# The 32 modulation products and their loads, moved from the convolutions into the attention

## The chip, the cores and the metric

The kernel runs on one core of a Trainium2 chip. The metric is the device time of one execution in microseconds (us), taken as the median of several runs. Beside the runs, one execution was recorded by the hardware profiler, and everything said below about where time goes comes from that record. The engines are TensorE (PE for its matmuls, PEld for its weight loads), VectorE (DVE), ScalarE (ACT), GpSimd (POOL) and SyncE (SP), whose instruction queue issues almost all DMA loads. [...]

## The reference, cut to what matters

One layer of a streaming encoder over 1024 positions of width 1024, in float32: an RMSNorm with modulation, a state-space (SSD) branch and a chunked attention branch side by side, an output projection with a gate, a second modulated norm and a convolutional feed-forward network with a gate.

```python
c_act = jax.nn.silu(c)
mod = (c_act @ w_ada[l] + b_ada[l])[:, None, :]
sh_m, sc_m, g_m, sh_f, sc_f, g_f = jnp.split(mod, 6, axis=-1)
h = rmsnorm(x, norm_mix_w[l]) * (1 + sc_m) + sh_m
z, xbc, dt_raw, q, k, v = jnp.split(h @ w_in[l], IN_SPLITS, axis=-1)
y_ssd = ssd_mixer(z, xbc, dt_raw, ...)
y_att = chunk_attention(q, k, v, rel_bias[l])
x = x + g_m * (jnp.concatenate([y_ssd, y_att], axis=-1) @ w_out[l])
h = rmsnorm(x, norm_ffn_w[l]) * (1 + sc_f) + sh_f
x = x + g_f * conv_ffn(h, w_up[l], ffn_conv_w[l], w_down[l])
```

The row of interest is `mod`: a vector of 1024 times a matrix of 1024 x 6144. Its six parts are two shifts, two scales and two gates. The first norm needs `sh_m` and `sc_m`; the other four (`g_m`, `sh_f`, `sc_f`, `g_f`) are needed only much later, the gate of the output projection first.

## The kernel before, in words

Every large product is made from pairs of numbers: a value is split into a rounded high part and a remainder (`split`, lines 60 to 66), and `mm3` (lines 55 to 58) adds three matmuls. `split` puts the high part on ACT (L65) and the remainder on DVE or POOL (L66).

**The modulation.** The vector by matrix product isn't made on TensorE. `w_ada` is stored as 48 blocks of 128 output columns by 1024; `mod_col(ft, t)` loads block `ft` (512 KB) into a tile `t` (L112, on SP's queue) and multiplies it on DVE with the activated `c`, held as a row in all partitions (`rowa`), summing along the row into one column of `modc` (L113). `mod_scale` and `mod_shift` (L168 to L174) turn a column into the scale `affn` and the shift `bffn` with three operations on 128 x 1 elements. Sixteen blocks (`sh_m`, `sc_m`) are done at the start, tile names `adat`. The other 32, tile name `mt`, are those of this change: 24 stand in `mods(kt)` after each of the eight convolutions, and the last eight (`g_f`) follow ahead of the z projection.

**The stages around the change**, with their places in the profiled execution:

- The first projection (to about 100 us) makes q, k and v of head pairs 0 and 1.
- The attention (about 100 to 325 us). `attention(p)` handles a pair of heads in four steps u, of two query blocks each. `attn_scores` makes the scores of one block in PSUM (L305, tile `s`, two buffers, one for each head), then per head one DVE operation that adds the bias and takes the row maximum (L317, tile `p`), the exponential on ACT (L320), and on DVE a reciprocal (L322) and the scaling (L323). `attn_pv` transposes the result on PE (L349, L352, tile `tp`), splits it (tile `pt`), multiplies by v (L360, L361, tile `pv`) and adds on DVE (L366, tile `ya`). The projections of pairs 2 and 3 (`gemm_part`, tile `acc`, six parts of 48 matmuls) are given as work between: three parts in pair 1, three in pair 2. Their weights are loaded into `raws` (L128) and split by ACT and POOL. Pairs 0 and 3 have no such part written into them.
- The convolutions (`conv_silu`, about 280 to 394 us): eight projections of 48 matmuls into the `s` tiles, each followed by ACT (L411) and three DVE operations that read the `s` tile (L413), and two more DVE operations (L419). The `s` tile is free for the next projection but one when these are done.
- The z projection (`z_tile`, tiles `zps` and `s`, about 384 to 442 us) with weights `wzh`, `wzl` made by ACT and DVE (L62, L63), the rows of the two gates (`row_of`, L120 to L124), the step sizes (`dt_prep`) and the first chunk of the SSD (`ssd_pre`, tiles `cb`, `rm`, `th`).
- Then the SSD chunks and the output projection (to about 600 us), and the feed-forward network.

**What sets the order.** A scheduler takes the instructions in the order in which they are written, estimates when each could run, and writes one list for each engine. Priorities follow the written order; a pin (`tc.issue_after(ins)`) forces an instruction behind `ins` in the list of that engine and adds no wait. The tiles `mt` come from a pool of three buffers (`MTB`), in memory that the attention's tiles hold before.

## Time and profile before

| | |
|---|---|
| median of 3 runs | 1265.64 us (1264.97 to 1270.69) |
| the profiled execution's own time | 1264.52 us |
| its span, first to last instruction | 1262.8 us |
| PE busy, DVE busy, ACT busy, POOL busy | 95%, 77%, 44%, 8% of the span |
| mean granted TensorE clock | 0.987 |
| the 32 products `mt` | first issue of a load at 326.3 us, last product at 415.7 us |

A row of the groups gives line, engine, operation, tile names, shapes and count, then busy us, mean ns of one, and the idle time of the engine before them with what ended it. A row of the waits reads: who waited, for whom, us in total, times, longest. A row of the windows gives, for a stretch from A to B, its length, the busy us of PE, PEld, DVE, ACT and POOL with their counts, the granted clock, the DMA share and GB/s. A row of the timeline gives start, length, engine, line, operation and tiles. "PE busy" counts a matmul until its modelled end, so a stretch in which matmuls wait can still look busy.

### The profile page before, as it was taken

What the parts mean: (1) busy time and instruction counts of PE and PEld (TensorE: products, weight loads), DVE (VectorE), ACT (ScalarE), POOL (GpSimd) and SP (SyncE); (2) the same over time, 40 slices, a digit from 0 to 9 for tenths busy, and PEclk for the clock granted to TensorE, in tenths of its full rate; (3) what the DMA queues carried; (4) which work ended last, traced back from release to release, by engine and by line L of the source; (5) the groups of instructions that cost most, each with busy time, mean ns of one, the idle gap of its engine ahead of it and who ended that gap; (6) DMA issues with size and microseconds to landing.
All of it is one profiled execution on the core that took longest, in us unless ns stands there. A gap on an engine that the chain in (4) does not pass through costs nothing.

```text
span 1262.8 us, 15592 instructions
## 1 busy us (share of the span) xinstructions
PE 1194.4 (95%) x5882; PEld 991.1 (78%) x5882; DVE 975.9 (77%) x1517; ACT 550.7 (44%) x901; POOL 105.2 (8%) x114
## 2 busy tenths in 40 slices
PE   5899999999999879999799999999999999999995
PEld 3777888878779768888578888888888888888884
DVE  7827665584797986664989898888998879856976
ACT  4516454563323443434634444443344435443443
POOL 1300201001200242310000000000000000000002
PEclk9999999899999989999999999999999999999998
DMA  9601110001574422212213323223322186834433
GB/s 341 245 1 42 42 42 33 29 1 34 186 249 150 133 84 67 67 67 67 89 46 125 125 75 108 92 100 126 125 76 106 75 311 217 301 108 140 160 125 133
DMA packets 55275, 146.67 MB, mean 116 GB/s; under 512 B 5280, under 2 KB 5408, under 8 KB 53792
## 3 DMA queue, kind: packets, MB, share of 16 engines
q1 hardware_dynamic: 48144, 121.30, 28.2%
q10 hardware_dynamic: 7056, 24.38, 4.8%
q8 instruction: 46, 0.75, 0.2%
q14 instruction: 29, 0.24, 0.1%
HBM read 116.56 MB, written 29.10 MB: 115 GB/s over the span
## 4 chain that ended last, share of the span: by engine, by line
PE 80%; DVE 13%; DMA 3%; ACT 2%; issue 1%; POOL 1%; DVEq 0%; POOLq 0%; SPq 0%; ACTq 0%
PE dn L57 6%; PE dn L56 6%; PE dn L58 5%; PE uY L56 5%; PE uY L58 5%; PE uY L57 5%; PE acc L57 3%; PE acc L56 3%; PE uZ L58 3%; PE uZ L56 3%; PE uZ L57 3%; PE acc L58 3%; PE uX L58 3%; PE uX L56 3%; PE uX L57 3%; PE s L305 3%
## 5 line engine op out<-in xcount | busy, mean ns | idle before, releaser
L56 PE MATMUL dn<-w 128*128 128x512 f32 x308 | 111.9, 389 | 0.0
L57 PE MATMUL dn<-w 128*128 128x512 f32 x308 | 111.9, 389 | 0.0
L58 PE MATMUL dn<-w 128*128 128x512 f32 x308 | 103.3, 389 | 0.0
L65 ACT ACTIVATE w<-ya 128x1024 fp32r<-128x1024 f32 (+1 forms) x44 | 41.8, 949 | 99.6 <-PE uY L58 92.2
L763 POOL TENSOR_TENSOR st<-st,mhalf 128x1 f32<-128x1 f32 x16 | 12.4, 777 | 680.0 <-DVE st L762 680.0
L56 PEld LDWEIGHTS dn<-w 128*128 128x128 f32 x308 | 57.8, 188 | 12.0
L58 PEld LDWEIGHTS dn<-w 128*128 128x128 f32 x308 | 57.8, 188 | 12.0
L57 PEld LDWEIGHTS dn<-w 128*128 128x128 f32 x308 | 57.8, 188 | 11.9
L66 DVE TENSOR_TENSOR pt<-tp,pt 128x512 fp32r<-128x512 f32 (+2 forms) x72 | 42.2, 595 | 28.1 <-ACT pt L65 28.0
L65 ACT ACTIVATE w<-xs 128x1024 fp32r<-128x1024 f32 (+1 forms) x44 | 41.8, 951 | 40.6 <-PE uY L58 31.6
L65 ACT ACTIVATE pt<-tp 128x512 fp32r<-128x512 f32 (+2 forms) x72 | 36.6, 523 | 45.6 <-PE tp L349 16.4
L56 PE MATMUL s<-hth,wh 128*128 128x512 f32 x128 | 50.8, 397 | 4.4 <-DVE xst L413 2.2
L317 DVE CUSTOM_DVE_ANT_0 p<-s,bias 128x640 f32<-128x640 f32 (+4 forms) x64 | 40.4, 649 | 16.2 <-PE tp L352 7.5
L66 DVE TENSOR_TENSOR w<-ya,w 128x1024 fp32r<-128x1024 f32 (+1 forms) x44 | 47.7, 1084 | 4.5 <-ACT w L65 4.5
L905 DVE SCALAR_TENSOR_TENSOR a<-cv,pkt,a 128x1023 f32<-128x1023 f32 (+1 forms) x40 | 51.0, 1276 | 0.1
L57 PE MATMUL s<-htl,wh 128*128 128x512 f32 x128 | 50.4, 394 | 0.0
L58 PE MATMUL s<-hth,wl 128*128 128x512 f32 x128 | 50.2, 392 | 0.0
L66 POOL TENSOR_TENSOR wl<-raws,wh 128x1024 fp32r<-128x1024 f32 x14 | 34.3, 2454 | 185.8 <-ACT wh L65 168.2
L320 ACT ACTIVATE p<-p,st 128x640 f32<-128x640 f32 (+4 forms) x64 | 44.1, 690 | 12.9 <-DVE st L317 12.6
L905 DVE SCALAR_TENSOR_TENSOR a<-cg,pkt,a 128x1023 f32<-128x1023 f32 (+1 forms) x40 | 49.5, 1276 | 0.0
L305 PE MATMUL s<-qk 64*128 64x320 f32 (+4 forms) x288 | 47.6, 340 | 0.3 <-DVE st L317 0.2
L66 DVE TENSOR_TENSOR w<-xs,w 128x1024 fp32r<-128x1024 f32 (+1 forms) x44 | 47.6, 1081 | 0.0
(407 smaller groups left out, 3583.4 us busy)
## 6 DMA issues: line engine op xcount, KB each, us to landing
mt<-in_w_ada_dram SPq DMA_DIRECT2D x32, 512.0 KB, 4.2
gz<-a ACTq DMA_DIRECT2D x10, 1024.0 KB, 5.2
adat<-in_w_ada_dram SPq DMA_DIRECT2D x16, 512.0 KB, 5.9
ya<-in_w_up_dram SPq DMA_DIRECT2D x10, 768.0 KB, 4.0
xs<-in_w_up_dram SPq DMA_DIRECT2D x10, 768.0 KB, 4.1
raws<-in_w_ft_dram SPq DMA_DIRECT2D x14, 512.0 KB, 3.5
gy<-a ACTq DMA_DIRECT2D x10, 512.0 KB, 2.6
qk<-in_x_dram SPq DMA_DIRECT2D x8, 512.0 KB, 6.0
```

What stands on the lines that cost most here:

```text
L56: T.matmul(ps, lh, rh, start=start, stop=False, skip_group_check=more)
L57: T.matmul(ps, lh, rl, start=False, stop=False, skip_group_check=more)
L58: T.matmul(ps, ll, rh, start=False, stop=stop, skip_group_check=more)
L65: i = A.activation(hi, src, AF.Copy) if ehi is A else ehi.tensor_copy(hi, src)
L66: return i, elo.tensor_tensor(lo, src, f32(hi), ALU.subtract)
L305: T.matmul(st[h][:, 512 * pi:512 * pi + w], d[qn][r, i * P:(i + 1) * P], d[kn][r, j0 * P + a:j0 * P + a + w], start=ti == 0, stop=ti == 2)
L317: V.tensor_tensor_reduce(out=dst, in0=src, in1=bsl, scale=-1.0, scalar=3e38, op0=ALU.add, op1=ALU.min, accum_out=nm)
L320: A.activation(pv_, pv_, AF.Exp, scale=-1.0, bias=nm, accum_out=rs)
L763: G.tensor_tensor(r, ms, mhalf[:, 0:1], ALU.pow)
L905: V.scalar_tensor_tensor(a[:, j:S], c[:, 0:S - j], w[2 - j], a[:, j:S], op0=ALU.mult, op1=ALU.add)
```

## The change

`mods` and its pool move from the convolution stage into the attention. In each step u of each pair, after the two heads' `attn_pv`, two columns are done: pair p and steps 0 and 1 do the four columns of `kt` = 2p (scale and shift, then the two gates), steps 2 and 3 those of `kt` = 2p + 1. That makes eight in each pair and 32 in all. Each load is pinned in SP's list behind the second bias load of its pair (`sp`), each product in DVE's list behind the last softmax scaling of its step (`last_v`). The pool now stands on the left side of the memory, where its first three loads wait for no other tile, and is closed with the attention. The eight `g_f` columns no longer use the `rm` tiles. No computation is added or dropped.

```diff
--- before.py
+++ after.py
@@ -108,10 +108,13 @@
         rawc[0] += 1
         return raws[:, rawc[0] % 2, 0:n]
 
-    def mod_col(ft, t):
-        nc.sync.dma_start(t, w_ada[ft])
-        V.tensor_tensor_reduce(out=t, in0=t, in1=rowa, scale=1.0, scalar=0.0,
-                               op0=ALU.mult, op1=ALU.add, accum_out=modc[:, ft:ft + 1])
+    def mod_col(ft, t, at=None):
+        sp, v = at or (None, None)
+        with tc.issue_after(sp) if sp else ExitStack():
+            nc.sync.dma_start(t, w_ada[ft])
+        with tc.issue_after(v) if v else ExitStack():
+            V.tensor_tensor_reduce(out=t, in0=t, in1=rowa, scale=1.0, scalar=0.0,
+                                   op0=ALU.mult, op1=ALU.add, accum_out=modc[:, ft:ft + 1])
 
     def row_of(cols, dst, psp, tag, bufs, ones, tmp):
         for hh in range(2):
@@ -320,7 +323,7 @@
             A.activation(pv_, pv_, AF.Exp, scale=-1.0, bias=nm, accum_out=rs)
             rr = stat()
             V.reciprocal(rr, rs)
-            V.tensor_scalar(pv_, pv_, rr, None, op0=ALU.mult)
+            last_v[:] = [V.tensor_scalar(pv_, pv_, rr, None, op0=ALU.mult).ins]
             res.append(pt_)
         return res
 
@@ -367,12 +370,14 @@
                         pv[0:64, :].rearrange("p (a b) -> p a b", a=2),
                         tl.rearrange("p (a b) -> p a b", a=2), ALU.add)
 
+    last_v = []
+
     def attention(p, extra=()):
         extra = dict(extra)
         bt = []
         for h in range(2):
             t = bp.tile([P, 640], F32, tag="bias", name="bias")
-            nc.sync.dma_start(t, bias[2 * p + h])
+            sp = nc.sync.dma_start(t, bias[2 * p + h]).ins
             G.memset(t[0:64, 576:640], -1e30)
             G.memset(t[64:128, 0:64], -1e30)
             bt.append(t)
@@ -383,6 +388,7 @@
                 fn()
             for h in range(2):
                 attn_pv(p, u, h, pa[h], pb[h])
+            mods(2 * p + u // 2, u % 2, (sp, last_v[0]))
 
     def gemm_ft(wh, wl, outs, rh, rl):
         for hh in range(2):
@@ -418,6 +424,22 @@
             A.activation(th, dst[:, c], AF.Tanh)
             V.scalar_tensor_tensor(dst[:, c], th, 1.0, dst[:, c], op0=ALU.add, op1=ALU.mult)
 
+    es_m = ExitStack()
+    mtp = es_m.enter_context(tc.tile_pool(name="mtp", bufs=1, side="left", reuse_waits="tile"))
+
+    def mt_tile():
+        return mtp.tile([P, D], F32, tag="mt", bufs=MTB, name="mt")
+
+    def mods(kt, part, at):
+        if part == 0:
+            mod_col(SC_F + kt, mt_tile(), at)
+            mod_scale(affn, SC_F, NFFN, kt)
+            mod_col(SH_F + kt, mt_tile(), at)
+            mod_shift(bffn, SH_F, kt)
+        else:
+            mod_col(G_M + kt, mt_tile(), at)
+            mod_col(G_F + kt, mt_tile(), at)
+
     part = lambda p, w: (lambda: gemm_part(p, w))
     attention(0)
     for p in (1, 2):
@@ -425,6 +447,7 @@
         for w in GPL:
             gemm_part(p + 1, w)
     attention(3)
+    es_m.close()
     es_at.close()
 
 
@@ -463,28 +486,12 @@
     sgt = f32(sgtr)
     na = bcp.tile([P, 16], F32, name="na")[:, 0:8]
     es_t = ExitStack()
-    es_m = ExitStack()
-    mtp = es_m.enter_context(tc.tile_pool(name="mtp", bufs=1, side="right", reuse_waits="tile"))
-
-    def mt_tile():
-        return mtp.tile([P, D], F32, tag="mt", bufs=MTB, name="mt")
-
-    def mods(kt):
-        mod_col(G_M + kt, mt_tile())
-        mod_col(SC_F + kt, mt_tile())
-        mod_scale(affn, SC_F, NFFN, kt)
-        mod_col(SH_F + kt, mt_tile())
-        mod_shift(bffn, SH_F, kt)
-
     for g in range(2):
         conv_silu(4 + g, bt_[g], th512)
-        mods(2 * g)
         conv_silu(6 + g, ct_[g], th512)
-        mods(2 * g + 1)
     for ft in range(4):
         xt = bcp.tile([P, S], F32, tag="rm", bufs=2, name="xst")
         conv_silu(ft, xt, th512)
-        mods(4 + ft)
         for hh in range(2):
             tps = tp_tile()
             for j in range(4):
@@ -514,8 +521,6 @@
             split(wh, wl, t, A, V)
             ws += [(wh[:, 0:512], wl[:, 0:512]), (wh[:, 512:1024], wl[:, 512:1024])]
         return ws
-
-    es_m.close()
 
     def rm512():
         return bcp.tile([P, S], F32, tag="rm", bufs=2, name="gt")[:, 0:512]
@@ -577,8 +582,6 @@
             T.matmul(dps[:, 64 * i:64 * i + 64], m, sm["adt"], start=True, stop=True)
         A.activation(ex3, dps[:, 0:192], AF.Exp)
 
-    for kt in range(KT):
-        mod_col(G_F + kt, bcp.tile([P, S], F32, tag="rm", bufs=2, name="mt"))
     def hb(n, c):
         return sm[n][:, c * 8:c * 8 + 8].unsqueeze(2).to_broadcast([P, 8, 64])
 
```

Three places show what this does to the lists. Line numbers of the changed kernel are 3 higher from the middle of the helpers on and 5 higher in the attention: L116 is the product (L113 before), L320 the maximum (L317), L325 and L326 reciprocal and scaling (L322, L323), L114 the load `mt` (L112), L380 the load of the bias (L375), L131 the load of projection weights (L128).

**DVE, pair 0 of the attention, from the second block's reciprocals to the fourth block's maximum.** Before:

```order
L322 RECIPROCAL st_72<-st_72 128x1
L323 TENSOR_SCALAR p<-p,st_72 128x256
L317 ISA p,st_72<-s,bias 128x384
L317 ISA st_72 128x1
L317 ISA p,st_72<-s,bias 128x384
L317 ISA st_72 128x1
L66 TENSOR_TENSOR pt<-tp,pt 128x384
L317 ISA p,st_72<-s,bias 128x512
```

And now:

```order
L325 RECIPROCAL st_72<-st_72 128x1
L326 TENSOR_SCALAR p<-p,st_72 128x256
L116 ISA mt,modc<-mt,rows 128x1024
L116 ISA modc 128x1
L116 ISA mt,modc<-mt,rows 128x1024
L116 ISA modc 128x1
L320 ISA p,st_72<-s,bias 128x384
L320 ISA st_72 128x1
L320 ISA p,st_72<-s,bias 128x384
L320 ISA st_72 128x1
L66 TENSOR_TENSOR pt<-tp,pt 128x384
L171 TENSOR_TENSOR st_72<-modc,pkt 128x1
```

Two products and one read of the sum each now stand between the scaling of a step's second block (256 columns) and the maximum of the next step's first block (384 columns) before the list went straight from the scaling to the maximum. The operations on `st` and `bffn` (L171, L177 and L173, three for a `kt`) follow the products a few places later.

**SP's list from the bias loads of pair 0 on**, where `raws` are the projection weights and `mt` the modulation blocks. Before:

```order
L128 DMA raws<-in_w_ft_dram 128x1024 x4
L375 DMA bias<-in_bias_dram 128x640 x5
L128 DMA raws<-in_w_ft_dram 128x1024 x3
L375 DMA bias<-in_bias_dram 128x640 x2
L128 DMA raws<-in_w_ft_dram 128x1024 x3
L375 DMA bias<-in_bias_dram 128x640
```

And now:

```order
L131 DMA raws<-in_w_ft_dram 128x1024 x4
L380 DMA bias<-in_bias_dram 128x640 x2
L114 DMA mt<-in_w_ada_dram 128x1024 x3
L380 DMA bias<-in_bias_dram 128x640
L114 DMA mt<-in_w_ada_dram 128x1024 x5
L380 DMA bias<-in_bias_dram 128x640
L114 DMA mt<-in_w_ada_dram 128x1024
L380 DMA bias<-in_bias_dram 128x640
L114 DMA mt<-in_w_ada_dram 128x1024 x2
L131 DMA raws<-in_w_ft_dram 128x1024
L114 DMA mt<-in_w_ada_dram 128x1024 x4
L131 DMA raws<-in_w_ft_dram 128x1024
```

The weight loads that followed each other, held only by their own buffers, now have up to five `mt` loads ahead of them in the same list, and so has a pair's second bias load.

**DVE in the convolutions**, where L413 and L419 are the three products and the last step of a convolution before the change (L419 and L425 after it), `ct` and `xst` its results. Before:

```order
L413 SCALAR_TENSOR_TENSOR ct_2777<-s,pkt,ct_2777 128x1023
L170 SCALAR_TENSOR_TENSOR affn<-st_72,pkt 128x1
L113 ISA mt,modc<-mt,rows 128x1024
L113 ISA modc 128x1
L113 ISA mt,modc<-mt,rows 128x1024
L113 ISA modc 128x1
L413 SCALAR_TENSOR_TENSOR ct_2777<-s,pkt,ct_2777 128x1022
L168 TENSOR_TENSOR st_72<-modc,pkt 128x1
L174 TENSOR_TENSOR bffn<-modc,pkt 128x1
L113 ISA mt,modc<-mt,rows 128x1024
L113 ISA modc 128x1
L413 SCALAR_TENSOR_TENSOR ct_2777<-s,pkt,ct_2777 128x1021
```

And now:

```order
L419 SCALAR_TENSOR_TENSOR xst<-s,pkt,xst 128x1022
L419 SCALAR_TENSOR_TENSOR xst<-s,pkt,xst 128x1021
L63 SCALAR_TENSOR_TENSOR wzl<-raws,wzh 128x2x260 x2
L425 SCALAR_TENSOR_TENSOR xst<-th,xst 128x512 x2
L63 SCALAR_TENSOR_TENSOR wzl<-raws,wzh 128x2x260
L419 SCALAR_TENSOR_TENSOR xst<-s,pkt,xst 128x1023
L419 SCALAR_TENSOR_TENSOR xst<-s,pkt,xst 128x1022
L419 SCALAR_TENSOR_TENSOR xst<-s,pkt,xst 128x1021
```

Between two operations of a convolution there were up to two products and small operations on `affn` and `bffn`; now the operations of a convolution follow each other, with only weight splits (`wzl`) between them.

## The prediction

> **What bounds the kernel now.** I read the page's busy shares and chain first, then the windows by stage, then who waits for whom inside the two stages that the change touches, and last the timeline for single durations.
>
> ```profile
> PE 1194.4 (95%) x5882; PEld 991.1 (78%) x5882; DVE 975.9 (77%) x1517; ACT 550.7 (44%) x901; POOL 105.2 (8%) x114
> PE 80%; DVE 13%; DMA 3%; ACT 2%; issue 1%; POOL 1%; DVEq 0%; POOLq 0%; SPq 0%; ACTq 0%
> ```
>
> TensorE carries four fifths of the chain, and DVE most of the rest. Where that rest lies is seen in the windows: pair 0 of the attention, pairs 1 and 2, pair 3, the first convolutions, the later ones, the z projection, and the start of the SSD chunks.
>
> ```profile
> 100.00:131.00 31.00, 30.22 (x180) 23.55 (x181) 24.76 (x79) 18.16 (x46) 2.55 (x10) 1.00 0.14 47
> 131.00:243.00 112.00, 110.88 (x631) 90.97 (x629) 63.65 (x171) 53.53 (x123) 12.51 (x9) 0.97 0.09 30
> 243.00:283.00 40.00, 38.16 (x242) 31.49 (x241) 36.67 (x109) 29.19 (x71) 2.67 (x3) 0.96 0.06 23
> 283.00:324.00 41.00, 41.00 (x226) 35.18 (x226) 15.61 (x22) 12.94 (x21) 5.37 (x3) 1.00 0.08 26
> 324.00:394.00 70.00, 64.99 (x326) 54.25 (x325) 68.36 (x113) 25.05 (x38) 10.13 (x7) 1.00 0.65 221
> 394.00:442.00 48.00, 44.04 (x337) 41.04 (x336) 39.80 (x78) 19.33 (x48) 7.31 (x4) 1.00 0.45 150
> ```
>
> The third number in each row that carries a bracket is DVE. It is full in two places: from 324 to 394 us (68.36 of 70), where the products are now, and in pair 3 of the attention (36.67 of 40). It is nearly full in pair 0 (24.76 of 31). Its large reserve is in pairs 1 and 2, 112 - 63.65 = 48.3 us, and in the first convolutions. The chain of waits from 322 to 420 us names the products and their loads first:
>
> ```profile
> by line: DVE mt L113 29.5%; DMA mt<-in_w_ada_dram 19.7%; DVE xst L413 8.6%; DVE bt L419 4.7%; DVE bt L413 3.8%; DVE ct L413 3.7%; issue 2.7%; PE zps L57 2.6%; DVE ct L419 2.5%; DVE xst L419 2.5%; PE zps L56 2.0%; PE zps L58 1.9%; PE s L56 1
> ```
>
> Half of it, 49%, is theirs. That isn't what their removal is worth, since PE works beside that chain. The worth is the time in which PE waited. These are PE's waits between 324 and 480 us:
>
> ```profile
> PE sg L613 <- ACT th L615: 3.3, 1, 3.3
> PE s L56 <- DVE xst L413: 2.2, 1, 2.2
> PE s L56 <- DVE ct L413: 2.1, 1, 2.1
> PE tp L613 <- DVE cb L600: 2.1, 1, 2.1
> ...
> PE zps L57 <- DVE wzl L63: 1.7, 2, 1.4
> PE wops L58 <- DVE yl L66: 1.7, 1, 1.7
> ...
> PE zps L56 <- ACT wzh L62: 0.4, 1, 0.4
> PE s L56 <- DVE affn L170: 0.3, 1, 0.3
> ```
>
> So a stage whose chain belongs to DVE for 100 us makes PE wait for a dozen of them.
>
> **What leaves the convolutions: a gain.** The products occupy DVE there for 29.00 and 9.86 us, 48 and 16 records for 24 and 8 products, since each has a read of its sum:
>
> ```profile
> 324.00:394.00 70.00, 29.00 (x48) 1.00 0.65 221
> 394.00:442.00 48.00, 9.86 (x16) 1.00 0.45 150
> ```
>
> Without them DVE has 68.36 - 29.00 = 39.4 us of work in the 70 us, and PE becomes the bound. The two waits of 2.2 and 2.1 us for a convolution's `s` tile go, because its three operations no longer stand behind products, and so does the 0.3 us behind `affn`: 4.6 us. The 2.1 us for `cb`, the first SSD chunk made ready inside the z projection, goes too: DVE reaches the step sizes late there because the last products and their loads stand ahead. Of the 1.7 + 0.4 us for z weights I take half, 1.0 us: the second set is split into buffers that the first set's last matmuls release, which stays. Sum 7.7, taken as 8 us. At least the 4.6 us go; at most every row above goes, 13.8 us. The loads' waits cost nothing more by themselves.
>
> **What enters the attention: a loss.** Back to back, a product takes 334.16 - 333.01 = 1.15 us of DVE's time, the read of the sum hidden in it; a column operation's row is 0.15 us.
>
> ```profile
> 333.01 1.22 DVE L113 CUSTOM_DVE_ANT_0 mt<-mt,rows 128x1024 f32<-128x1024 f32 x1
> 334.16 1.22 DVE L113 CUSTOM_DVE_ANT_0 mt<-mt,rows 128x1024 f32<-128x1024 f32 x1
> 353.28 0.15 DVE L174 TENSOR_TENSOR bffn<-modc,pkt 128x1 f32<-128x1 f32 x1
> ```
>
> Each step now ends with a block of 2.3 us between its last scaling and the next step's maximum. Behind the block stand that maximum, which frees the `s` tiles for PE's next scores, and the low halves `pt`, for which PE's value products wait. What covers the block differs by pair, so I count them by place.
>
> *Pair 0*, six blocked products (steps 0 to 2) and six column operations: 6 x 1.15 + 6 x 0.15 = 7.8 us. In pair 0 DVE waits in all for
>
> ```profile
> DVE p L317 <- PE s L305: 2.8, 2, 2.5
> DVE v L66 <- ACT v L65: 1.6, 2, 1.1
> DVE st L322 <- ACT p L320: 0.3, 1, 0.3
> ```
>
> and the first two lie ahead of the first product, so nothing covers the blocks: no projection matmuls are written into this pair for PE to do meanwhile. I take 7.5 us; with all of the remaining idle, 31 - 24.76 - 2.8 = 3.4 us, used, it is 4.4. Its last two products, after step 3, fall into a wait that exists already and cost nothing:
>
> ```profile
> 131.85 0.29 DVE L317 CUSTOM_DVE_ANT_0 p<-s,bias 128x128 f32<-128x128 f32 x1 [2.13 <-issue]
> ```
>
> PE runs a projection there; were it done sooner, they would cost up to their 2.3 us.
>
> *Pair 3*, eight products (the two after pair 2's last step and those of steps 0 to 2) and six column operations: 8 x 1.15 + 0.9 = 10.1 us. DVE's idle there is 40 - 36.67 = 3.3 us. Two of its waits are
>
> ```profile
> DVE pt L66 <- ACT pt L65: 1.9, 3, 1.0
> DVE ya L366 <- ACT tl L365: 0.7, 2, 0.5
> ```
>
> none longer than 1.0 us, so blocks of 2.3 us fill them in part: I take 8 us, between 6.8 (all idle used) and 10.1. The last two products come after the last scaling, when PE is on the first convolutions and DVE has work for 15.61 of 41 us: nothing.
>
> *Pairs 1 and 2*, the other 14 products, 16.1 us into 48.3 us of idle. Most of that idle is in long pieces while PE runs projections:
>
> ```profile
> DVE ya L366 <- ACT tl L365: 17.5, 7, 4.4
> DVE pt L66 <- ACT pt L65: 14.8, 9, 5.6
> ```
>
> So the products are covered by PE's projections. What isn't covered is a low half `pt` that PE wants just behind a block. I take 2 us for seven blocks, between 0 and 8 (half of their time).
>
> Sum of the loss: 7.5 + 8 + 2 = 17.5 us. From SP's side the loads are hidden: a load of 512 KB lands in 4.2 us (first row below), three buffers are ahead, and a step, which takes two of them, lasts over 7 us (31 / 4 in pair 0). The weight loads behind them in SP's list stood some 21 us apart before (second row, the span of three):
>
> ```profile
> mt<-in_w_ada_dram SPq DMA_DIRECT2D x32, 512.0 KB, 4.2
> 135.29 42.73 SPq L128 DMA_DIRECT2D raws<-in_w_ft_dram  x3
> ```
>
> [...] In the convolutions a 0.15 us operation took 1.45 us, until POOL's weight split ended:
>
> ```profile
> 345.66 2.38 POOL L66 TENSOR_TENSOR wl<-raws,wh 128x1024 fp32r<-128x1024 f32 x1 [8.03 <-ACT wh L65]
> 346.61 1.45 DVE L170 SCALAR_TENSOR_TENSOR affn<-st,pkt 128x1 f32<-128x1 f32 x1
> ```
>
> POOL's 12.51 us in pairs 1 and 2 are five such splits (5 x 2.38 = 11.9) and little else, and there DVE has room. [...]
>
> **The sum.** 17.5 - 8 = +9.5 us on the profiled execution's 1264.52 us, which is 1274.0. The median of the runs is 1.1 us above that execution, so 1275 us for the median.
>
> **Rivals.**
>
> *The attention absorbs the blocks (faster).* If PE keeps fed in pair 0 because the new list does more transposes and value products before the next pair, only pair 3 costs, at its low end of 6.8 us, and the gain is at its high end of 13.8: -7.0 us, 1259 us. It decides at a loss below 7.5 us, 13.8 less the 6.3 us that are 0.5%. For it speaks the 48 us of idle in pairs 1 and 2; against it that DVE is full in pairs 0 and 3, and lag on a full PE can't be regained. 11%.
>
> *A draw.* Loss at its low ends, 4.4 + 6.8 + 0 = 11.2, and a gain of 8 to 13.8: between -2.6 and +3.2, 1266 us. 17%.
>
> *The clock falls in the pauses (slower still).* After a pause of 1.1 us in pair 2 the granted clock was half for some 7 us:
>
> ```profile
> PE pv L361 <- DVE pt L66: 2.2, 4, 1.1
> ...
> 217.00:220.00 3.00, 1.88 (x14) 1.37 (x10) 3.00 (x5) 1.38 (x5) 1.35 (x1) 0.91 0.20 57
> 220.00:223.00 3.00, 3.00 (x10) 2.39 (x9) 2.48 (x8) 2.41 (x6) 0.00 (x0) 0.50 0.32 117
> 223.00:227.00 4.00, 4.00 (x12) 3.12 (x11) 2.96 (x8) 0.92 (x2) 0.00 (x0) 0.59 0.00 0
> ```
>
> That is 1.5 + 1.6 = 3.1 us of PE lost. Six blocks outside pairs 1 and 2 make pauses of this kind; three episodes more would add 9 us: 1284 us. Against it: pauses of 2 us in the convolutions left the clock at 1.00. [...] 13%.
>
> *SP's list holds weights back.* A weight load stands behind a `mt` load whose buffer frees only after a product; if three of the six come late by a load, 4.2 us each, it is 9.5 + 12.6 = +22 us, 1288 us. Against it the 20 us between loads. 4%.
>
> **How the numbers follow.** The forecast, +9.5 and between +4 and +16 (losses between low and high end, gain 8), has 55%. A difference of 0.5%, 6.3 us, is about what a measurement of this kernel tells from none. Slower by more: 0.47 of the forecast's 0.55, 0.13 of the clock, 0.04 of the queue, 0.02 of the draw, 0.66. Within: 0.08 + 0.15 = 0.23. Faster: 0.11. The range reaches from 1262 (inside the absorbing case) to 1286 (past three clock episodes): it leaves out part of the first and the late weights.
>
> **What the changed profile would show.** Right: no PE wait over 1 us for L419 and none for `cb`; DVE over 90% busy in pairs 0 and 3; pair 0's stretch to the first maximum of pair 1 some 7 us longer, pair 3's some 8 us; pairs 1 and 2 within 3 us of before; products at 1.2 us there with no wait for a load. Wrong: a pair 0 of the same length, products waiting for loads, PE waits of 2 us that stay in the convolutions with another releaser, or long waits for `raws`.

## The result and the profile after

The changed kernel takes 1281.81 us (median, 1277.80 to 1284.11) and the kernel before, run beside it, 1265.66 us. The ratio is 1.0111, with a 95% interval of 1.0082 to 1.0140: slower by 14 us, between 10 and 18. The forecast was 1275 us. Two profiled executions of the experiments below (`e1_none`, `e10_conv32`) ran at a mean granted clock of 0.751 and 0.845, where the timed ones had 0.939 to 0.988, and one execution of `e5_single` took 4160.9 us, so no duration is taken from these three.

These are the page's busy times, its chain and its row of the loads, after the change; the profiled execution, the fastest of the five, took 1277.8 us, its span is 1276.1 us:

```profile
PE 1200.3 (94%) x5882; PEld 997.8 (78%) x5882; DVE 975.6 (76%) x1517; ACT 552.3 (43%) x901; POOL 105.3 (8%) x114
PE 80%; DVE 12%; ACT 3%; issue 2%; DMA 2%; POOL 0%; SPq 0%; DVEq 0%; POOLq 0%; ACTq 0%
...
mt<-in_w_ada_dram SPq DMA_DIRECT2D x32, 512.0 KB, 4.1
```

DVE's total is unchanged (975.9 before), and so are its instructions: the same work stands elsewhere. To see where the 13 us between the two spans arise, I use marks on PE that both traces have: the first scores against a single block of keys (`64x128`), with which each pair begins, and the first matmul of the convolutions. Timeline of PE, before, then after (start, length, engine, line, operation):

```profile
100.50 0.33 PE L305 MATMUL s<-qk 64*128 64x128 f32 x2
124.19 0.32 PE L305 MATMUL s<-qk 64*128 64x128 f32 x1
247.39 0.32 PE L305 MATMUL s<-qk 64*128 64x128 f32 x1
279.33 0.44 PE L56 MATMUL s<-hth,wh 128*128 128x512 f32 x1
```

```profile
100.05 0.33 PE L308 MATMUL s<-qk 64*128 64x128 f32 x2
135.21 0.32 PE L308 MATMUL s<-qk 64*128 64x128 f32 x1
257.94 0.32 PE L308 MATMUL s<-qk 64*128 64x128 f32 x1
300.51 0.44 PE L56 MATMUL s<-hth,wh 128*128 128x512 f32 x1
```

Pair 0 is 23.7 us long before and 35.2 after, pairs 1 and 2 together 123.2 and 122.7, pair 3 31.9 and 42.6. From the first convolution to the end of the span it is 1262.8 - 279.33 = 983.5 us before and 1276.1 - 300.51 = 975.6 after. So the attention lost 21.6 us and the rest gained 7.9; with the start 0.4 us earlier, that is the 13.3 us between the spans.

The windows between these marks (length, then busy PE, PEld, DVE, ACT, POOL with counts, granted clock, DMA share, GB/s), before: pair 0, pairs 1 and 2, pair 3.

```profile
100.50:124.20 23.70, 22.92 (x143) 17.57 (x142) 19.21 (x65) 15.45 (x41) 0.95 (x6) 1.00 0.07 26
124.20:247.40 123.20, 122.08 (x693) 100.23 (x692) 73.09 (x195) 60.56 (x138) 16.49 (x14) 0.97 0.11 33
247.40:279.30 31.90, 30.06 (x197) 24.80 (x197) 28.98 (x89) 22.09 (x56) 0.29 (x2) 0.95 0.07 27
```

After, the same three, and then the stretch of 70 us in the convolutions that answers to 324 to 394 us before, shifted by the lag of 21 us:

```profile
100.00:135.20 35.20, 30.07 (x164) 24.52 (x162) 30.42 (x90) 16.25 (x42) 1.00 (x6) 0.81 0.39 136
135.20:257.90 122.70, 116.42 (x667) 94.90 (x666) 90.83 (x229) 58.83 (x133) 17.26 (x14) 0.99 0.31 101
257.90:300.50 42.60, 35.12 (x201) 29.11 (x201) 41.06 (x117) 23.85 (x60) 0.29 (x2) 0.80 0.36 120
...
345.00:415.00 70.00, 70.00 (x381) 60.65 (x380) 39.54 (x51) 27.09 (x43) 8.71 (x7) 1.00 0.13 39
```

In pair 0 DVE's busy time grew by 11.2 us (19.21 to 30.42) and the pair by 11.5: DVE had no reserve there. In pair 3 it grew by 12.1 and the pair by 10.7; DVE is 96% busy. In pairs 1 and 2 it grew by 17.7 and nothing got longer. In the convolutions DVE fell from 68.36 to 39.54 us of 70, and PE, 64.99 before, is full. PE's waits from 300 to 490 us say the same (who waited, for whom, us in total, times, longest):

```profile
PE sg L616 <- ACT th L618: 3.3, 1, 3.3
PE wops L56 <- ACT yh L65: 1.9, 1, 1.9
PE wops L58 <- DVE yl L66: 1.7, 1, 1.7
PE ydp L678 <- DVE th L619: 0.4, 1, 0.4
PE tp L616 <- DVE cb L603: 0.4, 1, 0.4
```

The waits for `xst`, `ct`, `affn` and the z weights are gone; `cb` fell from 2.1 to 0.4.

### The profile page after: what moved, and what is told of

The parts are those of the page before. It is cut to its first block, busy times and chain, and to the rows that moved or that the text cites. A ratio compares the mean times of both kernels' runs of the same rounds, so it can differ in the third digit from the quotient of the medians.

```text
span 1276.1 us, 15577 instructions
## 1 busy us (share of the span) xinstructions
PE 1200.3 (94%) x5882; PEld 997.8 (78%) x5882; DVE 975.6 (76%) x1517; ACT 552.3 (43%) x901; POOL 105.3 (8%) x114
## 4 chain that ended last, share of the span: by engine, by line
PE 80%; DVE 12%; ACT 3%; issue 2%; DMA 2%; POOL 0%; SPq 0%; DVEq 0%; POOLq 0%; ACTq 0%
PE dn L56 5%; PE dn L57 5%; PE dn L58 5%; PE uY L56 5%; PE uY L58 5%; PE uY L57 5%; PE uZ L57 3%; PE uZ L58 3%; PE uZ L56 3%; PE uX L56 3%; PE uX L57 3%; PE uX L58 3%; PE acc L56 3%; PE acc L57 3%; PE s L56 3%; PE s L57 3%
## 5 line engine op out<-in xcount | busy, mean ns | idle before, releaser
L58 PEld LDWEIGHTS dn<-w 128*128 128x128 f32 x308 | 57.8, 188 | 12.1
L323 ACT ACTIVATE p<-p,st 128x640 f32<-128x640 f32 (+4 forms) x64 | 44.1, 690 | 28.1 <-DVE st L320 27.7
L908 DVE SCALAR_TENSOR_TENSOR a<-cv,pkt,a 128x1023 f32<-128x1023 f32 (+1 forms) x40 | 51.0, 1276 | 0.1
L66 DVE TENSOR_TENSOR pt<-tp,pt 128x512 fp32r<-128x512 f32 (+2 forms) x72 | 41.8, 595 | 10.7 <-ACT pt L65 10.2
L320 DVE CUSTOM_DVE_ANT_0 p<-s,bias 128x640 f32<-128x640 f32 (+4 forms) x64 | 40.0, 649 | 10.9 <-PE s L308 6.3
```

What stands on the lines that cost most here:

```text
L58: T.matmul(ps, ll, rh, start=False, stop=stop, skip_group_check=more)
L66: return i, elo.tensor_tensor(lo, src, f32(hi), ALU.subtract)
L320: V.tensor_tensor_reduce(out=dst, in0=src, in1=bsl, scale=-1.0, scalar=3e38, op0=ALU.add, op1=ALU.min, accum_out=nm)
L323: A.activation(pv_, pv_, AF.Exp, scale=-1.0, bias=nm, accum_out=rs)
L908: V.scalar_tensor_tensor(a[:, j:S], c[:, 0:S - j], w[2 - j], a[:, j:S], op0=ALU.mult, op1=ALU.add)
```

## The experiments

The marks give one table for all runs but `e1_none` and `e10_conv32`: us in each part, the attention's sum, from the first convolution to the end of the span, and the time in which PE had half clock within the attention (from the trace's clock record).

| run | median us | pair 0 | pairs 1, 2 | pair 3 | attention | rest | half clock |
|---|---|---|---|---|---|---|---|
| before | 1265.7 | 23.7 | 123.2 | 31.9 | 178.8 | 983.5 | 10 |
| after | 1281.8 | 35.2 | 122.7 | 42.6 | 200.5 | 975.6 | 34 |
| e1_none | 1254.7 | | | | | | |
| e4_thin | 1253.1 | 23.8 | 121.4 | 31.1 | 176.3 | 972.0 | 3 |
| e13_halfsize | 1263.8 | 27.4 | 126.0 | 33.6 | 187.0 | 970.8 | 17 |
| e2_no_ends | 1261.8 | 23.7 | 126.5 | 33.4 | 183.6 | 972.1 | 7 |
| e3_no_middle | 1270.2 | 37.2 | 112.5 | 37.3 | 187.1 | 972.2 | 27 |
| e5_single | 1269.9 | 31.4 | 119.8 | 40.8 | 192.0 | 973.8 | 20 |
| e9_warm | 1275.8 | 34.7 | 124.3 | 41.2 | 200.2 | 973.2 | 7 |
| e6_lo_dve | 1282.9 | 35.9 | 124.4 | 40.5 | 200.8 | 980.7 | 41 |
| e8_left | 1279.4 | 24.8 | 122.7 | 31.2 | 178.7 | 977.6 | 3 |
| e10_conv32 | 1264.6 | | | | | | |
| e12_mid_each | 1267.7 | 23.7 | 128.3 | 39.9 | 191.9 | 975.6 | 24 |
| e11_half | 1252.3 | 23.7 | 116.5 | 36.7 | 176.9 | 970.6 | 7 |

The median of the kernel before, taken again with each group of runs, was 1266.15, 1267.74 and 1266.66 us. Without their profiled execution the medians of `e1_none` and `e10_conv32` are 1254.2 and 1264.2 us.

### What is gained without a price: no products, and products of 8 elements

In `e1_none`, `mod_col` returns at once for the 32 columns, which are filled instead:

```diff
+    V.tensor_copy(modc[:, 16:32], modc[:, 0:16])
+    V.tensor_copy(modc[:, 32:48], modc[:, 0:16])
```

> Left out: all 32 products and their loads; the 32 columns are filled by two copies of the first sixteen columns, while the column operations (affn, bffn) stay in the attention. What is left is the gain with no price. Theory (the products leave a loaded stage worth 8 us and cost about 20 us in pairs 0 and 3): 1257 us, 8 below before; 1261 if only the waits behind conv tiles go, 1252 if every listed wait goes. Rival (the changed order itself, column operations and pins, costs): 1265 us or more.

In `e4_thin`, the loads and pins stay and the product is cut:

```diff
-            V.tensor_tensor_reduce(out=t, in0=t, in1=rowa, scale=1.0, scalar=0.0,
+            n = 8 if at else D
+            V.tensor_tensor_reduce(out=t[:, 0:n], in0=t[:, 0:n], in1=rowa[:, 0:n], scale=1.0, scalar=0.0,
```

> Changed size: all 32 loads of 512 KB, pins and column operations stay, but a product reads only 8 of the 1024 elements of each row (so most of each sum is left out), some 0.1 us instead of 1.15. Theory (DVE's time in the blocks is the price, loads are free): within 2 us of the kernel without products, about 1259 us. Rival (loads in SP's list hold the weights or biases back, or the pinned order costs): stays at 1275 to 1282 us.

Measured: 1254.7 us (ratio 0.9915, 0.9890 to 0.9940) and 1253.1 us (0.9907, 0.9878 to 0.9937). The gain is 11 to 13 us and not 8. And the 32 loads of 512 KB with their pins, all within the attention, cost nothing that can be seen: with them the kernel is no slower than without. The rival that SP's list holds weights back is out. The whole price comes with the length of the products on DVE.

### Where the price arises: products left out by pair

`e2_no_ends` leaves out the products of pairs 0 and 3 as shown here, `e3_no_middle` those of pairs 1 and 2, with `(1, 2)` in the same place:

```diff
     def mods(kt, part, at):
+        sk = kt // 2 in (0, 3)
         if part == 0:
-            mod_col(SC_F + kt, mt_tile(), at)
+            mod_col(SC_F + kt, mt_tile(), at, sk)
```

> Left out: the 16 products and loads of pairs 0 and 3 (their columns are filled by copies); the 16 of pairs 1 and 2 stay as in the changed kernel. Theory (the loss lies in pairs 0 and 3, where no projection covers a block): within 2 us of the kernel without any product, about 1258 to 1260 us. Rival (the products of pairs 1 and 2 pay too, held up by POOL's weight splits): 1266 us or more.

> Left out: the 16 products and loads of pairs 1 and 2 (columns filled by copies); those of pairs 0 and 3 stay. Theory: nearly all of the loss stays, 1278 to 1282 us. Rival (weight splits and products in pairs 1 and 2): 1270 us or less. If the two places simply share the loss by count, this and the run without pairs 0 and 3 come out alike, near 1270 us.

Measured: 1261.8 us (0.9966, 0.9944 to 0.9988) and 1270.2 us (1.0032, 1.0004 to 1.0059). Over the 1254.7 us without products, the 16 of pairs 1 and 2 cost 7.1 us alone, the 16 of pairs 0 and 3 15.5 us, and all 32 together 27.1. The ends cost twice the middle, but both runs miss the theory's ranges (1258 to 1260 and 1278 to 1282 us): the middle isn't free, and the ends alone don't make nearly all of the loss. Both together cost 4.5 us more than the two alone. By the ratios the three prices are 6.5, 14.8 and 24.8 us, an excess of 3.5, and the intervals leave about 4 us of doubt on each, so the medians alone don't show it; by the table it is 6.1 us: attention +7.3, +10.8 and +24.2 us over the thin products.

It also suggests why. With pairs 1 and 2 free of products of their own (`e3_no_middle`) these take 112.5 us, 8.9 less than with thin products: they pay back most of the 13.4 us that pair 0 lost. With their own products on DVE (122.7 after) they can't. The windows from pair 1's first scores to pair 3's, `e2_no_ends` first, then thin products:

```profile
124.30:250.80 126.50, 121.09 (x693) 98.74 (x692) 91.92 (x240) 61.34 (x139) 16.61 (x14) 0.99 0.30 101
```

```profile
125.80:247.20 121.40, 119.48 (x693) 97.72 (x692) 75.61 (x243) 60.67 (x139) 15.48 (x14) 0.99 0.31 107
```

DVE is idle for 34.6 us of the 126.5, and still the stretch is 5.1 us longer. PE's longest wait there stands behind a single block, whose second product took 3.36 us instead of 1.22 (timeline of DVE, then PE):

```profile
221.65 3.36 DVE L118 CUSTOM_DVE_ANT_0 mt<-mt,rows 128x1024 f32<-128x1024 f32 x1
225.74 0.79 PE L56 MATMUL acc<-hth,wh 128*128 128x512 f32 x1 [2.99 <-DVE qk L66]
```

Its length is that of the two products that ran beside a weight split on POOL in the changed kernel, 3.36 and 3.38 us (see the section on POOL's splits below). The next longest wait, 1.7 us, stands behind a block of the usual length. What PE waits for is one operation behind one block, not DVE's sum.

### How the price grows with the time of a product, and with its place

`e13_halfsize` is `e4_thin` with `n = D // 2`.

> The changed kernel with products that read 512 of the 1024 elements (half of each sum is left out; loads whole), some 0.6 us each, so a block takes 1.2 instead of 2.3 us at the same places. Theory (the loss follows the time a block holds DVE up): half way between the kernel with thin products (1253) and the changed kernel (1282), 1265 to 1270 us. Rival (up to a length a block is hidden by the waits for ACT and PE, beyond it each microsecond costs): 1254 to 1260 us.

Measured: 1263.8 us (0.9975, 0.9960 to 0.9991), 11 us over thin products and 18 under the changed kernel: just under the theory's 1265. Half a product takes 0.68 us instead of 1.22 (56%) and costs 11 of 29 us (37%): a part of the shorter block is hidden, but not all of it, as the rival had.

`e5_single` puts one product behind each query block's last scaling:

```diff
             pa = attn_scores(p, 2 * u, bt)
+            first = last_v[0]
             pb = attn_scores(p, 2 * u + 1, bt)
...
-            mods(2 * p + u // 2, u % 2, (sp, last_v[0]))
+            mods(2 * p + u // 2, u % 2, (sp, first), (sp, last_v[0]))
```

> All 32 products stay, but one stands behind each query block's last scaling (blocks of 1.15 us, twice as many) instead of two behind every second. Theory (DVE's total time in pairs 0 and 3 is the price): as the changed kernel within 4 us, 1278 to 1286 us, pair 0 some 34 us long. Rival (the length of a block makes the pauses in which PE loses its clock): 1265 to 1272 us, pair 0 some 28 us long, half clock in pairs 0 and 3 below 7 us in all instead of 27.

Measured: 1269.9 us (1.0011, 0.9993 to 1.0029), 12 us less than the changed kernel with the same products in the same pairs. The theory in the form "DVE's total time is the price" is wrong by this run. The rival named the right time, and its cause isn't settled: half clock in pairs 0 and 3 fell from 30.7 to 13.7 us, where the rival had below 7, and pair 0 took 31.4 us instead of 28. Other things differ too. One is seen in DVE's groups in pair 0 (line, operation, tiles, shapes, count; busy us, mean ns; idle before them): scalings and low halves `pt` of the kernel before,

```profile
L323 DVE TENSOR_SCALAR p<-p,st 128x640 f32<-128x640 f32 (+4 forms) x12 | 5.1, 435 | 0.2
L66 DVE TENSOR_TENSOR pt<-tp,pt 128x384 fp32r<-128x384 f32 (+1 forms) x6 | 3.5, 589 | 0.0
```

of the changed kernel,

```profile
L116 DVE CUSTOM_DVE_ANT_0 mt<-mt,rows 128x1024 f32<-128x1024 f32 x6 | 7.1, 1219 | 0.0
L326 DVE TENSOR_SCALAR p<-p,st 128x640 f32<-128x640 f32 (+4 forms) x14 | 6.4, 457 | 0.4
L66 DVE TENSOR_TENSOR pt<-tp,pt 128x384 fp32r<-128x384 f32 (+1 forms) x8 | 4.8, 618 | 0.0
```

and of `e5_single`:

```profile
L116 DVE CUSTOM_DVE_ANT_0 mt<-mt,rows 128x1024 f32<-128x1024 f32 x7 | 8.5, 1215 | 1.0 <-DMA mt<-in_w_ada_dram 1.0
L326 DVE TENSOR_SCALAR p<-p,st 128x640 f32<-128x640 f32 (+4 forms) x14 | 6.2, 449 | 0.2
L66 DVE TENSOR_TENSOR pt<-tp,pt 128x384 fp32r<-128x384 f32 (+1 forms) x6 | 3.5, 589 | 0.0
```

Before, two more scalings, two more low halves and one more `ya` of pair 0 came after pair 1's first scores, and so under pair 1's first projection. With blocks of two products they come ahead of it: 1.3 + 1.3 us for the scalings and low halves in these rows, which nothing covers any more. The scheduler writes the list anew with every change, and a longer block moved the tail of pair 0 out from under its cover. With single products half of that tail stays covered, in spite of one product more in the stretch. Another difference is a wait of DVE for the second block's scores, which a product fills in `e5_single`, where only a wait for that product's load is left (DVE's waits in pair 0, changed kernel, then `e5_single`):

```profile
DVE p L320 <- PE s L308: 2.6, 1, 2.6
```

```profile
DVE mt L116 <- DMA mt<-in_w_ada_dram: 1.0, 1, 1.0
```

And no product of `e5_single` takes longer than 1.23 us, where two of the changed kernel take 3.4 beside POOL. What each of these and the clock is worth in the 12 us, no run tells apart.

### The clock: more matmuls to fill the pauses

`e9_warm` adds matmuls whose result nobody reads, in pairs 0 and 3:

```diff
+    def warm(p, after):
+        if p in (1, 2):
+            return
+        ps = ps1.tile([P, 512], F32, tag="acc", bufs=1, name="warm")
+        with tc.issue_after(after.ins):
+            for _ in range(4):
+                T.matmul(ps, hth[:, 0, 0:P], hth[:, 0, 0:512], start=True, stop=True)
```

> The changed kernel with four more matmuls of 512 columns (some 0.25 us each, result unused) behind the scores of each query block of pairs 0 and 3, 64 in all, so that PE's pauses there are shorter. Theory (PE waits for DVE there, its clock matters little): the matmuls fill pauses, and the time stays within 4 us of the changed kernel, 1278 to 1286 us. Rival (half clock after pauses is a large part of the loss): half clock in pairs 0 and 3 falls from 27 us to below 7, and the time falls by 6 to 10 us, to 1272 to 1276.

The pauses in pairs 0 and 3 do lower the clock in the changed kernel: it was half for 13.7 us in pair 0 and for 17.1 in pair 3. The long stretch of half clock in pair 0 and the one in pair 3 of the changed kernel, and then the whole of pair 0 and pair 3 in `e9_warm`:

```profile
112.30:126.00 13.70, 12.86 (x58) 11.40 (x59) 13.39 (x38) 8.08 (x19) 0.00 (x0) 0.50 0.32 107
...
286.30:300.00 13.70, 13.13 (x61) 11.29 (x59) 13.48 (x39) 6.50 (x15) 0.00 (x0) 0.50 0.21 75
```

```profile
99.80:134.50 34.70, 32.82 (x185) 25.54 (x184) 32.41 (x98) 17.97 (x45) 1.62 (x10) 1.00 0.50 175
258.80:300.00 41.20, 35.23 (x233) 28.57 (x232) 38.96 (x112) 23.39 (x60) 0.29 (x2) 1.00 0.37 124
```

With the added matmuls the clock is 1.00 throughout both pairs, and pair 0 takes 34.7 instead of 35.2 us, pair 3 41.2 instead of 42.6, the attention as a whole 200.2 instead of 200.5. In the two stretches of half clock DVE is busy for 13.39 and 13.48 of 13.7 us, so for most of them PE waits for DVE at any clock. But the slow clock isn't free: at the end of pair 3 the chain of work that ended last runs over PE, whose twelve score matmuls take 2.67 us there and 1.54 in `e9_warm` (changed kernel first):

```profile
295.82 2.67 PE L308 MATMUL s<-qk 64*128 64x320 f32 x12
```

```profile
294.52 1.54 PE L316 MATMUL s<-qk 64*128 64x320 f32 x12
```

The pairs can't be compared cleanly, since the list changed with the added matmuls: eight products stand in pair 0 instead of six, and pairs 1 and 2 are 1.6 us longer. The median, 1275.8 us (1.0068, 1.0039 to 1.0096), is 6 us lower than the changed kernel's, in spite of the 64 matmuls more. That is inside the rival's range of 1272 to 1276 and below the theory's, so the theory that the clock matters little missed. The profiled executions differ by only 2.9 us in their spans, 2.4 of them after the first convolution; but the changed kernel's had a mean granted clock of 0.976, and its four others, with 0.968 to 0.972, took 3.9 to 6.3 us longer, while the five of `e9_warm` had 0.985 to 0.990. So some 6 us of the loss go with the clock. The two intervals overlap a little and no longer execution was traced, so neither the exact size nor the place is shown.

### Products beside POOL's weight splits

`e6_lo_dve` moves the low halves of the six weights of pairs 2 and 3 to DVE:

```diff
-        wh, wl = wu_pair(w_ft[8 + 3 * (p - 2) + which], A, G)
+        wh, wl = wu_pair(w_ft[8 + 3 * (p - 2) + which], A, V)
```

> The changed kernel with the low halves of the six weights of pairs 2 and 3 subtracted on DVE (1.1 us each) instead of POOL (2.4 us or more), so that no POOL split meets a product. Theory (DVE and POOL excluding each other is a small part: one or two products of 3.4 us): products all 1.2 us, time within 3 us of the changed kernel, 1279 to 1285 us. Rival (it is the price of the products in pairs 1 and 2): 5 to 8 us less than the changed kernel, 1273 to 1277 us.

In the changed kernel, products and weight splits do meet, twice. Timeline of the first meeting (POOL, then DVE, then PE, whose next matmul waits for the operation behind the product):

```profile
165.27 3.28 POOL L66 TENSOR_TENSOR wl<-raws,wh 128x1024 fp32r<-128x1024 f32 x1 [17.80 <-ACT wh L65]
166.27 3.36 DVE L116 CUSTOM_DVE_ANT_0 mt<-mt,rows 128x1024 f32<-128x1024 f32 x1
169.56 0.68 DVE L66 TENSOR_TENSOR qk<-acc,qk 128x512 fp32r<-128x512 f32 x1
170.30 0.80 PE L56 MATMUL acc<-hth,wh 128*128 128x512 f32 x1 [2.90 <-DVE qk L66]
```

The product takes 3.36 us instead of 1.22, and PE stands for 2.90 us. The times look as if the two ran in turn: the split, begun 1.0 us before the block's first product ended, takes 0.9 us longer than its usual 2.38, and the second product ends 1.1 us after the split (169.63 and 168.55 us), which is about its own length. What makes them do so no trace shows. The other one (215.00 us, 3.38 us) is alike, and PE's two long waits in pairs 1 and 2 of the changed kernel, 5.5 of 6.1 us in all, stand behind these two products:

```profile
PE acc L56 <- DVE qk L66: 2.9, 1, 2.9
PE acc L56 <- DVE st L171: 2.6, 1, 2.6
```

Without those splits the time was 1282.9 us (1.0128, 1.0099 to 1.0158), no less than with them. But six operations of 1.22 us came onto DVE in their place, and one product of 3.37 us was left beside the split of a convolution's weights, with a wait of PE of 2.92 us behind it; the theory had all products at 1.2 us. So the run shows that nothing is saved by this move, and not what the held-up products cost by themselves. The meetings are real, some 4.3 us of DVE's time in the changed kernel, and a part of the price of the 16 products in the middle: in `e2_no_ends` the one wait of 2.99 us behind a product of that length stands in a stretch that is 5.1 us longer. They aren't all of it, since the attention of `e12_mid_each` below has none and still costs more.

### Can the products stay with the convolutions?

`e8_left` is the kernel before with the pool of the loads on the other side of the memory:

```diff
+    mtp = es_m.enter_context(tc.tile_pool(name="mtp", bufs=1, side="left", reuse_waits="tile"))
...
-    mtp = es_m.enter_context(tc.tile_pool(name="mtp", bufs=1, side="right", reuse_waits="tile"))
```

> The kernel before with only the place of the three load buffers changed: on the side of the memory that the attention does not hold, so that the products stay in the convolutions but the first need not wait for the attention's memory. Theory (the gain comes from DVE no longer being full between 324 and 394 us): products start near 285 us, DVE has 84 us of work in the 111 us of the convolutions, and 6 to 10 of the 12 us of the gain come without a loss: 1255 to 1260 us. Rival (the products stay where they were in DVE's list, and the order decides): 1264 to 1268 us.

Measured: 1279.4 us (1.0104, 1.0072 to 1.0137). Neither theory had this. With nothing that held them back, the scheduler took the loads and 24 of the 32 products into the first projection. The windows of the products alone, and of that stage in this run, and then of that stage in the kernel before:

```profile
0.00:120.00 120.00, 31.87 (x24) 0.93 0.70 263
```

```profile
10.00:119.70 109.70, 89.87 (x368) 68.34 (x366) 87.11 (x175) 34.57 (x53) 16.47 (x15) 0.92 0.69 260
```

```profile
10.00:100.50 90.50, 79.86 (x368) 63.35 (x366) 58.50 (x118) 34.32 (x53) 14.48 (x15) 1.00 0.48 176
```

The attention begins 19.2 us late, and the stages behind it run well (178.7 and 977.6 us). Here the clock has a visible price: it falls to 0.92, and the same 368 matmuls keep PE busy for 10.0 us more. So the buffers' old place, which the attention holds, was also what kept the products from running early.

`e10_conv32` therefore pins them: loads behind pair 3's second bias load, products behind pair 3's last scaling, four behind each convolution.

> All 32 products after the attention again, four behind each convolution, but with the load buffers on the side of the memory that the attention does not hold, the loads pinned behind pair 3's second bias load and the products behind pair 3's last scaling. Theory (what held the kernel before back was that 32 products squeezed into the last 70 of the 111 us of convolutions made DVE full; what held the run with the moved buffers back was the products that came ahead of the attention): pairs 0 to 3 as long as before, products from some 285 us, and most of the 12 us of the gain: 1255 to 1260 us. Rival (DVE cannot take 37 us of products in that stage without making PE wait, wherever they start): 1263 to 1268 us.

Measured: 1264.6 us (0.9993, 0.9976 to 1.0010), no change, so the rival is borne out by the time: 32 products in that stage cost the gain, from whichever side they come. How PE waits there stays open.

### All in the middle, and the version that beats both

`e12_mid_each` has all 32 in pairs 1 and 2, two behind each query block:

```diff
+            if p in (1, 2):
+                mods(4 * (p - 1) + u, 0, (sp, first))
+                mods(4 * (p - 1) + u, 1, (sp, last_v[0]))
```

> All 32 products in pairs 1 and 2, two (2.3 us) behind each query block's last scaling, none in pairs 0 and 3. DVE's idle there was 48 us before and the products are 37. Theory (cover by projections decides): pairs 0 and 3 as long as before, pairs 1 and 2 up to 10 us longer, 1258 to 1266 us. Rival (blocks of two cost the same wherever they stand, 7 us for 16 in pairs 1 and 2): 14 us or more, 1268 us or more.

Measured: 1267.7 us (1.0009, 0.9993 to 1.0026), 13 us over no products: above the theory's 1258 to 1266 and close to the rival's 14. Pairs 1 and 2 take 6.9 us more than with thin products, and pair 3, in which the last four products of pair 2 now stand, 8.8 us more.

`e11_half` has one product behind each query block of pairs 1 and 2 (the two gates) and two behind each convolution (scale and shift), pinned as in `e10_conv32`:

```diff
+            if p in (1, 2):
+                mod_col(G_M + 4 * (p - 1) + u, mt_tile(), (sp, first))
+                mod_col(G_F + 4 * (p - 1) + u, mt_tile(), (sp, last_v[0]))
...
+    def mods_c(kt):
+        mod_col(SC_F + kt, mt_tile(), at_c)
+        mod_scale(affn, SC_F, NFFN, kt)
+        mod_col(SH_F + kt, mt_tile(), at_c)
+        mod_shift(bffn, SH_F, kt)
```

> The 16 products of the two gates in pairs 1 and 2, one behind each query block's last scaling; the 16 of scale and shift behind the convolutions, two each, from buffers that the attention does not hold. Theory (single products in pairs 1 and 2 are hidden by the projections, and the convolutions' DVE has room for 18 us): within 3 us of the kernel without products, 1254 to 1258 us, and faster than both kernels. Rival (each product in the attention costs its share, 7 us for 16): 1262 us or more.

Measured: 1252.3 us (0.9896, 0.9867 to 0.9925): as fast as without any product, 13 us faster than before and 29 faster than the change. Its windows from pair 1's first scores to pair 3's, to the first convolution, and 17 and 16 us within the first convolutions:

```profile
124.30:240.80 116.50, 115.57 (x681) 95.90 (x680) 86.15 (x219) 58.14 (x134) 15.68 (x14) 1.00 0.32 107
240.80:277.50 36.70, 33.03 (x210) 27.39 (x209) 33.42 (x100) 23.91 (x60) 0.29 (x2) 0.91 0.21 67
...
283.00:300.00 17.00, 17.00 (x93) 14.50 (x92) 15.51 (x33) 4.87 (x8) 2.40 (x1) 1.00 0.79 264
300.00:316.00 16.00, 16.00 (x87) 13.71 (x86) 15.94 (x33) 4.40 (x7) 2.43 (x1) 1.00 0.60 212
```

DVE is nearly full in those 33 us of the convolutions (31.4 us), and PE is full too: it waits for nothing. The stretch had some 25 us of DVE idle that neither kernel used. As many products in pairs 1 and 2 as cost 7.1 us in blocks of two (with 12 column operations beside them, and one of them held up by POOL) cost nothing that can be seen as single ones, none of them held up in the attention. By the marks pairs 1 and 2 are 4.9 us shorter than with thin products and pair 3 is 5.6 longer, so only their sum says this.

## Why the prediction was right, and where its sizes were off

The sign, the place and the mechanism held: the attention loses more than the convolutions gain, since pairs 0 and 3 have no DVE time to give. The forecast was +9.5 us over the profiled execution; the two spans differ by 13.3, the medians by 16.2, the ratio gives 14. Both sides of the sum were too small, the gain by 3.4 us and the loss by some 10 (27.1 against 17.5), and these errors in part cancel: that the time came out within 7 us is partly luck. Nor does the range of +4 to +16 follow from the bounds that are given for it: 11.2 - 8 is +3.2, and 7.8 + 10.1 + 8 - 8 is +17.9.

**The gain, 8 us.** Without any product the medians give 11.4, so this term was low by 3.4; the range of 4.6 to 13.8 held it. In the changed kernel itself, from the first convolution on, 7.9 us are seen. The rest is larger by 3.6 us than with thin products (975.6 and 972.0); what that is was not found.

**Pairs 0 and 3, 7.5 + 8 = 15.5 us.** Alone, their 16 products cost 15.5 us (`e3_no_middle` less `e1_none`). That this equals the sum of the two terms is chance: by the marks of that run pair 0 is 13.4 us longer than with thin products and pair 3 6.2, and pairs 1 and 2 are 8.9 shorter. By the marks of the changed kernel it looks larger, 11.5 and 10.7, and both are outside the bounds I gave (7.8 and 10.1). In pair 0 the difference is work of the pair itself, which used to lie under pair 1's projection and now stands ahead of it. My step counted only what the change writes into the pair, and not what the new list takes out from under a cover elsewhere.

**Pairs 1 and 2, 2 us.** This is the step that failed. "So the products are covered by PE's projections" rests on DVE's idle time, 48 us; alone, the 16 products cost 7.1 us there, near the upper bound of 8, and together with those of pairs 0 and 3 perhaps some 4 more, since pairs 1 and 2 could have paid back what pair 0 lost. A sum of prices by place missed that. What PE waits for there isn't a low half `pt`, as the step had it, but the operation that reads a projection's result out of `acc` (`qk`), above all behind a product that a POOL split holds up. `e11_half` shows that the cover is there, for blocks half as long.

**The rivals.** The clock fell in the pauses, as that rival had it: half clock for 24 us more than before. Its price of 9 us is not refuted: with the clock raised by added matmuls the median falls by 6 us, so this is a part of the loss and not all of it, since `e9_warm` is still 8 us slower than the kernel before. In the profiled execution less of it is seen, 200.2 instead of 200.5 us of attention. That rival counted three short episodes more, each with 3.1 us of PE lost; in the traces half clock lies in stretches of 13.7, 3.4, 3.4 and 13.7 us in the attention of the changed kernel, and of 6.8 and 3.4 us in that of the kernel before. Beside POOL's splits two products were held up, 2.1 us each. That DVE has room where they meet was no cover: PE waits 2.9 and 2.6 us behind them. SP's list held nothing back: loads landed in 4.1 us, and thin products with all loads cost nothing. The attention didn't absorb the blocks; single products in pairs 1 and 2 it does (`e11_half`).

**What the profile was to show.** Right: no wait for the convolutions' tiles, products of 1.2 us that wait for no load (but for the two beside POOL), pairs 1 and 2 within 3 us of before, DVE over 90% in pair 3. Not right: DVE is 86% busy in pair 0 and not over 90 (81% before), since it waits for the same first scores; pairs 0 and 3 grew by 11 us and not by 7 and 8; a wait of 0.4 us for `cb` is left.

## What to carry to other kernels

Idle time of an engine in a stage is not yet room for more work: what counts is how long one piece holds up the next operation that another engine waits for, so spread such work in single pieces between the waits, see what else can hold a piece up (here a POOL operation beside the second of two products, which took 3.36 us instead of 1.22), and look for a stage in which the other engine has long runs of its own (here the first convolutions). Price a moved block by what the new list puts ahead of the next cover, not by the block alone, and don't add up prices of neighbouring stages when one of them pays back the other's lag. A buffer that comes free late can be what keeps work from running too early; whoever frees it has to put a pin in its place.

## What was not expected of the hardware

A product of 128 x 1024 on VectorE beside a POOL subtraction took 3.36 and 3.38 us instead of 1.22, and the POOL operation 3.28 and 2.95 instead of 2.38 us: both took longer where they met. Of half clock on TensorE, the two stretches of 13.7 us lie where VectorE is busy for 98% of the time, and the profiled execution shows little of a price; yet with the clock at 1.00 there the median fell from 1281.8 to 1275.8 us, and the executions of one and the same kernel that had the lower mean clock were the longer ones (1277.8 us at 0.976, 1284.1 at 0.968).
